# Output projection's right half in groups (0, 1), (2), (3), and the last tile's expert rows accumulated in DRAM onto a stored shift

## The chip, the cores and the metric

The kernel runs on one core of a Trainium2 chip. A core has a matrix engine (PE), three engines for elementwise work (DVE, ACT, POOL), a queue engine that issues most transfers here (SP), and 16 DMA engines. Each engine works through its own list of instructions in order, and waits on semaphores where it needs another one's result. The metric is the device time of one launch, in microseconds (us); the time before is the median of three runs.

## What is computed

One layer with a conditioning vector c: a token mixer (convolution, gated recurrence, linear attention) whose output goes through a projection `w_out`, and then a mixture of 16 experts, of which each token uses two. 512 tokens, width 1024, float32.

```python
        mod = (c_act @ w_ada[l] + b_ada[l])[:, None, :]
        sh1, sc1, gt1, sh2, sc2, gt2 = jnp.split(mod, 6, axis=-1)
        h = rms_norm(x, g_mix[l]) * (1.0 + sc1) + sh1
        x = x + gt1 * token_mix(h, w_in[l], conv_dw_w[l], conv_dw_b[l], conv_ln_g[l], conv_ln_b[l],
...
        h = rms_norm(x, g_ffn[l]) * (1.0 + sc2) + sh2
        x = x + gt2 * hier_moe(h, w_route_group[l], b_route_group[l], w_route_expert[l],
                               b_route_expert[l], w_gate[l], w_up[l], w_down[l])
    return rms_norm(x, g_final)
```

`token_mix` ends in `mixed @ w_out`, the output projection. `hier_moe` picks one of four groups by `h @ w_rg`, two of its four experts by `h @ w_re`, and adds their outputs `(silu(h w_gate) * (h w_up)) w_down`, weighted.

## The kernel before

**Tiles and stages.** The 512 tokens stand in four tiles of 128 (NT = 4). A first stage normalises x and runs the mixer; up to some 220 us this is not touched. Then come the output projection with the routing, from about 200 to 262 us, and the experts, to the end.

**Output projection.** Its 1024 output columns are done in two halves. The left half (`ps0`) is done for all four tiles. The right half is done by `project(tiles, units)`: it goes through the eight steps of 128 input columns, at each step three matmuls for each tile in `tiles` (`mm3`, L84 to L86: products of high and low parts), the last three steps together tile by tile. After each step it may run one of `units`, that is, other work that is written in between. `yres(i, half, ps)` multiplies a finished half by the gate (tile yr, L981) and adds it to the residual xt(i) (L982), both on DVE.

**Routing of a tile.** `route_half(i, hf)` scales half a tile of xt into xa (L997, DVE), transposes it by PE (tile ph2, L1001), copies it on ACT (h2t, L1003), multiplies it by the routing weights on PE (pl, L1006) and copies that on ACT (pls, L1008). `route(i)` does this for the right half, stores xt(i) in DRAM (xo_rows, L1029, SP), squares and sums xt(i) on ACT (L1031, result in ss2), takes the power -1/2 of the mean (a scaling on DVE L116, a power on POOL L117), sums the four partial logits on PE (L1035) and writes the tile's logits lg (L1036, DVE).

**Rows for the experts.** `rows(i)` makes h of tile i, that is xa times the root mean square factor plus the shift sh2, and stores it in DRAM as h2_dram (h2_rows in the lists, h_rows in the trace; L1045, SP). For tiles 0 to 2 that is one DVE instruction (L1041); for the last tile it is a multiplication on ACT (L1043) and an addition on POOL (L1044):

```python
        else:
            nc.scalar.mul(xa, xa, ss2[:, i:i + 1])
            nc.gpsimd.tensor_tensor(xa, xa, sh2, ALU.add)
        nc.sync.dma_start(h2_dram[i * P:(i + 1) * P, :], xa)
```

**From logits to experts.** With all four tiles' lg, DVE finds each token's group and experts by maxima and one-hot masks (`first_max`, L1103 to L1110), PE counts positions (L1134), and a list of row numbers is made for each expert (sidx, L134). POOL then gathers an expert's rows from DRAM (`gather`, L1142, tile gat), which needs h2_dram of all tiles and the expert's sidx. DVE also ranks the experts by load (L1175 to L1186), and all engines branch on whether one is overfull (L1290, L1291). After the branch PE transposes the gathered rows of the first expert (L1383), and the expert stage runs.

**Experts and their weights.** An expert has three weight matrices; all are streamed from DRAM in 96 chunks of 1 MB (`load_chunk`, L966, issued on SP) over a ring of 17 slots, in the order of use. A chunk's load waits until its slot is free and until the load three before it has landed (AHEAD = 3). Eight experts are computed one at a time in three-pass matmuls (L84 to L86), the other eight in pairs (L1414, L1460). The results are added to xo_rows in DRAM by indexed accumulating DMAs from POOL (L1086).

**What sets the order.** The source gives the order in which work is written; a scheduler then sets each engine's list. The lists around the change stand below as they come out.

Of the kernel before, what the change touches and what calls it, by code (L numbers as in the profile page):

```python
# [13 lines left out]
ALU = mybir.AluOpType  # L14
# [3 lines left out]
P = 128  # L18
D = 1024
T = 512  # L20
NT = T // P
# [27 lines left out]
def trunk_kernel(  # L49
# [7 lines left out]
    nc = tc.nc  # L57
# [9 lines left out]
    h2_dram = nc.dram_tensor("h2_rows", (T, D), F32, kind="Internal").ap()  # L67
# [9 lines left out]
    def big(name):  # L77
        return pbank("pz", 6, name)

    def small(name):  # L80
        return pbank("ps", 2, name)

    def mm3(ps, lh, ll, rh, rl, start, stop):
        nc.tensor.matmul(ps, lh, rh, start=start, stop=False)  # L84
        nc.tensor.matmul(ps, lh, rl, start=False, stop=False)  # L85
        nc.tensor.matmul(ps, ll, rh, start=False, stop=stop)  # L86
# [28 lines left out]
    def rstd_of(dst, src, n):  # L115
        nc.vector.tensor_scalar(dst, src, 1.0 / n, EPS, ALU.mult, ALU.add)  # L116
        return nc.gpsimd.tensor_tensor(dst, dst, mhalf[:, 0:dst.shape[1]], ALU.pow)  # L117
# [256 lines left out]
    for kd in range(KD):  # L374
# [10 lines left out]
        if kd in (1, 2, 4):  # L385
            n = kd // 2 + 1
# [74 lines left out]
    def t512(name, tag="t", bufs=8):  # L461
        return tmp.tile([P, T], F32, tag=tag, bufs=bufs, name=name)
# [317 lines left out]
    def row_tile(name):  # L780
        return modp.tile([P, D], F32, tag="row", name=name)

    def bcast(dst, row):
        nc.sync.dma_start(dst, row.rearrange("(o n) -> o n", o=1).broadcast_to((P, D)))
# [4 lines left out]
    gt1, a2, sh2 = (row_tile(n) for n in ("gt1", "a2", "sh2"))  # L789
# [4 lines left out]
    def mod_rows():  # L794
        nc.sync.dma_start(wr[:, :, 0:4], w_route_group[0].rearrange("(k p) g -> p k g", p=P))
        for g in range(4):
            nc.sync.dma_start(wr[:, :, 4 + 4 * g:8 + 4 * g],
                              w_route_expert[0, g].rearrange("(k p) e -> p k e", p=P))
        nc.sync.dma_start(br[:, 0:4], b_route_group)
        nc.sync.dma_start(br[:, 4:20], b_route_expert[0].rearrange("g e -> (g e)").rearrange("(o g) -> o g", o=1))  # L800
        bcast(gt1, mod_dram[0])
        bcast(a2, mod_dram[2])
        bcast(sh2, mod_dram[1])
        nc.sync.dma_start(sh2r, mod_dram[1].rearrange("(k p) -> k p", p=P))
        for hf in range(2):
            cols = slice(hf * 512, hf * 512 + 512)
            gffn = t512(f"gffn{hf}")
            nc.sync.dma_start(gffn, g_ffn[:, cols].broadcast_to((P, 512)))
            nc.vector.scalar_tensor_tensor(a2[:, cols], a2[:, cols], 1.0, gffn, ALU.add, ALU.mult)
# [85 lines left out]
    def w_right():  # L895

        for n, kd in enumerate(ksteps):
            if kd not in right:
                if n < 6:
                    if n % 2 == 0:  # L900
                        both_ = ring0[n // 4].tile([P, 2, 2, 512], F32R, tag="raw", name=f"parts_o{kd}")
                    hi, lo = both_[:, n % 2, 0, :], both_[:, n % 2, 1, :]
                else:
                    hi = wop.tile([P, 512], F32R, tag="wh", name=f"hi_r{kd}")
                    lo = wop.tile([P, 512], F32R, tag="wl", name=f"lo_r{kd}")
                split(hi, lo, rawo[1, kd])
                right[kd] = hi, lo
            yield kd, *right[kd]
# [69 lines left out]
    def yres(i, half, ps):  # L978
        t = late.tile([P, 512], F32, tag="yr", bufs=1, name=f"yr{half}{i}")
        cs_ = slice(half * 512, half * 512 + 512)  # L980
        nc.vector.tensor_tensor(t, ps, gt1[:, cs_], ALU.mult)  # L981
        nc.vector.tensor_tensor(xt[i][:, cs_], xt[i][:, cs_], t, ALU.add)  # L982
# [10 lines left out]
    def route_half(i, hf):  # L993

        xa = xas[i]
        cols = slice(hf * 512, hf * 512 + 512)
        nc.vector.tensor_tensor(xa[:, cols], xt[i][:, cols], a2[:, cols], ALU.mult)  # L997
        pt = big(f"ph2{i}{hf}")
        for kk in range(4):
            k = hf * 4 + kk  # L1000
            nc.tensor.transpose(pt[:, kk * P:(kk + 1) * P], xa[:, k * P:(k + 1) * P], ident)  # L1001
        h2t = late.tile([P, 4, P], F32, tag="h2t", bufs=2, name=f"h2t_{i}{hf}")
        nc.scalar.copy(h2t, pt.rearrange("p (k t) -> p k t", k=4))  # L1003
        pl = small(f"pl{i}{hf}")
        for q in range(4):
            nc.tensor.matmul(pl[32 * q:32 * q + 32, 0:P], wr[:, hf * 4 + q, :], h2t[:, q, :], start=True, stop=True)  # L1006
        pls[i, hf] = late.tile([P, P], F32, tag=f"pls{hf}", bufs=1 if hf else NT, name=f"pls{i}{hf}")
        nc.scalar.copy(pls[i, hf], pl[:, 0:P])  # L1008

    def project(tiles, units=()):  # L1010

        py = {i: big(f"py1{i}") for i in tiles}
        units, held = list(units), []
        for n, step in enumerate(w_right()):
            held.append(step)
            if KD - 3 <= n < KD - 1:
                continue
            for i in tiles:
                for kd, hi, lo in held:
                    mm3(py[i], mth[:, kd, i * P:(i + 1) * P], mtl[:, kd, i * P:(i + 1) * P],  # L1020
                        hi, lo, kd == first, kd == final)
            held = []
            if units:
                units.pop(0)()
        return py

    def route(i):
        route_half(i, 1)
        nc.sync.dma_start(xo_dram[i * P:(i + 1) * P, :], xt[i])  # L1029
        junk = late.tile([P, D], BF16, tag="junk2", bufs=1, name=f"junk2{i}")  # L1030
        nc.scalar.activation(junk, xt[i], AF.Square, accum_out=ss2[:, i:i + 1])  # L1031
        rstd_of(ss2[:, i:i + 1], ss2[:, i:i + 1], D)
        pl2 = small(f"pl2{i}")
        for hf in range(2):
            nc.tensor.matmul(pl2[:, 0:20], pls[i, hf], sel, start=(hf == 0), stop=(hf == 1))  # L1035
        nc.vector.scalar_tensor_tensor(lg[:, i, :], pl2[:, 0:20], ss2[:, i:i + 1], lgc, ALU.mult, ALU.add)  # L1036

    def rows(i):
        xa = xas[i]
        if i < NT - 1:  # L1040
            nc.vector.scalar_tensor_tensor(xa, xa, ss2[:, i:i + 1], sh2, ALU.mult, ALU.add)  # L1041
        else:
            nc.scalar.mul(xa, xa, ss2[:, i:i + 1])  # L1043
            nc.gpsimd.tensor_tensor(xa, xa, sh2, ALU.add)  # L1044
        nc.sync.dma_start(h2_dram[i * P:(i + 1) * P, :], xa)  # L1045

    for i in range(NT):
        yres(i, 0, ps0[i])
    py = project((0, 1))
    for i in range(2):  # L1050
        yres(i, 1, py[i])
    py = project((2, 3), [lambda i=i: [route_half(n, 0) for n in (i, i + 1)] for i in (0, 2)]
                 + [lambda i=i: route(i) for i in (0, 1)])
    for i in range(nring - 8, EARLY):
        load_chunk(i)
    for i in (0, 1):
        rows(i)
    for i in range(2, NT):
        yres(i, 1, py[i])
        route(i)  # L1060
    for i in range(2, NT):
        rows(i)
    keep_busy(10)
# [602 lines left out]
```

## Time and profile before

| | |
|---|---|
| median of 3 runs | 544.02 us (541.79 to 544.24) |
| profiled execution, its own time | 539.03 us |
| its span in the trace | 537.3 us |
| PE busy | 505.9 us, 94% |
| DVE busy | 362.5 us, 67% |
| ACT busy | 248.5 us, 46% |
| POOL busy | 90.0 us, 17% |
| DMA, HBM read | 156.35 MB, 314 GB/s over the span |
| mean granted clock of PE | 0.977 of full speed |

Rows below come from the one profiled execution. Times are us from the start of its span, line numbers are those of the kernel before. "Idle before" in brackets is the time for which an engine stood still ahead of an instruction, with the work that ended it. A q behind an engine's name means its queue: a waiting or issuing instruction, not counted as busy.

### The profile page before, as it was taken

How to read it: one execution, taken by the hardware profiler on the slowest of the kernel's cores; microseconds unless marked ns; L12 is line 12 of the kernel's file. 1: busy time of each engine (PE TensorE's matmuls, PEld its weight loads, DVE VectorE, ACT ScalarE, POOL GpSimd, SP SyncE). 2: the span in 40 equal slices, each digit the busy share in tenths (PEclk: the TensorE clock that was granted, in tenths of full speed). 3: DMA queues.
4: the chain of work that ended last, by engine and by line, in shares of the span. 5: the costliest groups of instructions: out<-in, count | busy, mean ns of one | idle time of the engine just before them, and what ended most of it. 6: DMA issues, size and time to landing. Idle time of an engine off the chain costs nothing. (4 is left out here: it accounts for less than half of the span.)

```text
span 537.3 us, 7963 instructions
## 1 busy us (share of the span) xinstructions
PE 505.9 (94%) x2835; PEld 344.5 (64%) x2835; DVE 362.5 (67%) x654; ACT 248.5 (46%) x397; POOL 90.0 (17%) x126
## 2 busy tenths in 40 slices
PE   8999999999998999996889999999999999999991
PEld 7766766677666887775667778787777353343341
DVE  4644499999988756538799999999899031120237
ACT  5432587496126543225467667777766011000113
POOL 3310414000025100104200211120120110112002
PEclk9999999999999999997599999999999999999997
DMA  8995978747727399368898899999999999999973
GB/s 284 300 344 151 290 252 282 231 155 302 291 77 267 154 359 421 160 234 294 314 351 305 321 371 360 352 375 366 348 391 373 363 412 357 393 365 402 403 323 156
DMA packets 54304, 164.58 MB, mean 306 GB/s; under 512 B 12181, under 2 KB 30881, under 8 KB 39926
## 3 DMA queue, kind: packets, MB, share of 16 engines
q1 hardware_dynamic: 50710, 156.36, 79.1%
q0 software_dynamic: 3552, 7.69, 5.4%
q8 instruction: 23, 0.38, 0.3%
q14 instruction: 19, 0.16, 0.1%
HBM read 156.35 MB, written 12.62 MB: 314 GB/s over the span
## 5 line engine op out<-in xcount | busy, mean ns | idle before, releaser
L509 DVE SCALAR_TENSOR_TENSOR cacc<-upad,vt,cacc 128x512 f32<-128x512 f32 x60 | 43.0, 753 | 0.1
L1537 DVE SCALAR_TENSOR_TENSOR sact<-pup,swt,sact 128x512 f32<-128x512 f32 x12 | 8.9, 745 | 49.7 <-PE pup L1414 49.7
L90 DVE TENSOR_TENSOR ml_u<-raw_u,mh_u 128x1024 fp32r<-128x1024 f32 x32 | 39.1, 1224 | 3.9 <-ACT mh_u L89 3.8
L89 ACT CAST mh_g<-raw_g 128x1024 fp32r<-128x1024 f32 x32 | 33.5, 1051 | 17.0 <-PE pga L86 12.3
L90 DVE TENSOR_TENSOR ml_g<-raw_g,mh_g 128x1024 fp32r<-128x1024 f32 x32 | 38.3, 1219 | 1.3 <-ACT mh_g L89 1.1
L89 ACT CAST mh_u<-raw_u 128x1024 fp32r<-128x1024 f32 x32 | 33.6, 1050 | 11.4 <-PE pga L86 9.2
L90 DVE TENSOR_TENSOR ml_d<-raw_d,mh_d 128x1024 fp32r<-128x1024 f32 x26 | 31.7, 1223 | 4.0 <-ACT mh_d L89 3.6
L1142 POOL DMA_INDIRECT gat<-h_rows,sidx x12 | 13.5, 1122 | 120.9 <-PE pgt L1383 68.9
L1460 PE MATMUL pd<-raw_d,ht 128*64 128x512 f32 x128 | 32.7, 599 | 0.9 <-DMA raw_d<-in_w_down_dram 0.9
L89 ACT CAST mh_d<-raw_d 128x1024 fp32r<-128x1024 f32 x26 | 27.3, 1049 | 8.1 <-PE pup L86 6.1
L1414 PE MATMUL pup<-raw_u,xh 128*64 128x512 f32 x128 | 29.4, 595 | 0.8 <-DMA raw_u<-in_w_up_dram 0.8
L1487 DVE TENSOR_TENSOR ye<-pd,gt 128x512 f32<-128x512 f32 x22 | 15.0, 690 | 20.9 <-PE pd L1460 19.4
L1414 PE MATMUL pga<-raw_g,xh 128*64 128x512 f32 x128 | 28.3, 594 | 0.0
L84 PE MATMUL pga<-mh_g,xh 128*128 128x512 f32 x64 | 27.6, 431 | 0.5 <-ACT xh L89 0.5
L85 PE MATMUL pup<-ml_u,xh 128*128 128x512 f32 x64 | 25.6, 400 | 1.6 <-DVE ml_u L90 1.5
L85 PE MATMUL pga<-ml_g,xh 128*128 128x512 f32 x64 | 26.2, 410 | 0.6 <-DVE ml_g L90 0.6
L86 PE MATMUL pga<-mh_g,xl 128*128 128x512 f32 x64 | 25.6, 400 | 0.4 <-DVE xl L90 0.4
L84 PE MATMUL pup<-mh_u,xh 128*128 128x512 f32 x64 | 25.8, 403 | 0.0
L86 PE MATMUL pup<-mh_u,xl 128*128 128x512 f32 x64 | 25.2, 394 | 0.0
L1086 POOL DMA_INDIRECT xo_rows<-ye,sidx x8 | 17.1, 2138 | 36.7 <-DVE ye L1487 36.7
L1460 PEld LDWEIGHTS pd<-raw_d,ht 128*64 128x64 f32 x128 | 10.6, 136 | 19.6 <-issue 16.0
L1426 ACT COPY ht<-pht 128x512 f32<-128x512 f32 x4 | 2.3, 587 | 42.6 <-PE pht L1422 42.6
(405 smaller groups left out, 1267.7 us busy)
## 6 DMA issues: line engine op xcount, KB each, us to landing
raw_g<-in_w_gate_dram SPq DMA_DIRECT2D x32, 1024.0 KB
raw_u<-in_w_up_dram SPq DMA_DIRECT2D x32, 1024.0 KB
raw_d<-in_w_down_dram SPq DMA_DIRECT2D x32, 1024.0 KB
wb<-in_w_ada_dram SPq DMA_DIRECT2D x16, 1024.0 KB
wa<-in_w_ada_dram SPq DMA_DIRECT2D x8, 512.0 KB
wa<-in_w_ada_dram SPq DMA_DIRECT2D x4, 1024.0 KB
raw_o<-in_w_out_dram SPq DMA_DIRECT2D x8, 512.0 KB
xin<-in_x_dram SPq DMA_DIRECT2D x4, 512.0 KB
```

The costliest lines, as they stand in the source:

```text
L84: nc.tensor.matmul(ps, lh, rh, start=start, stop=False)
L85: nc.tensor.matmul(ps, lh, rl, start=False, stop=False)
L86: nc.tensor.matmul(ps, ll, rh, start=False, stop=stop)
L89: one = nc.scalar.copy(hi, src)
L90: two = nc.vector.tensor_tensor(lo, src, hi.bitcast(F32), ALU.subtract)
L509: nc.vector.scalar_tensor_tensor(cacc[:, h, :], upad[:, h, t:t + T], w, cacc[:, h, :], ALU.mult, ALU.add)
L1086: nc.gpsimd.indirect_dma_start(out=xo_dram, out_offset=bass.IndirectOffsetOnAxis(ap=si, axis=0), in_=y, in_offset=None, bounds_check=T - 1 ...
L1142: return g, nc.gpsimd.indirect_dma_start(out=g, out_offset=None, in_=h2_dram, in_offset=bass.IndirectOffsetOnAxis(ap=sidx[:, e:e + 1], axi ...
L1414: nc.tensor.matmul(ps[rows_of(a)], xh[:, k, rows_of(a)], raws[used[0] + a][:, kk, :], start=(k == 0), stop=(k == KD - 1))
L1460: nc.tensor.matmul(ps[hf][rows_of(a)], ht[:, k, rows_of(a)], raws[used[0] + k // 2 * 2 + a][:, k % 2, cols(hf)], start=(k == 0), stop=(k = ...
L1487: nc.vector.tensor_tensor(y[:, cols], ps[hf], gt2[:, cols], ALU.mult)
L1537: nc.vector.scalar_tensor_tensor(sa, pu, swt[:, u:u + 1], sa, ALU.mult, ALU.mult)
```

## The change

Three things. The shift sh2 is stored once in the last tile's part of h2_dram, early (`mod_rows`). The last tile's rows are no longer completed on POOL and stored by SP: after ACT's multiplication POOL issues a DMA that adds them onto what stands in DRAM. And the right half is projected for tile 2 and tile 3 one after the other, with other units of routing written between their steps; yres(2, 1) is written ahead of tile 3's projection, and the logits of tile 2 inside it.

```diff
--- before.py
+++ after.py
@@ -801,6 +801,8 @@
         bcast(gt1, mod_dram[0])
         bcast(a2, mod_dram[2])
         bcast(sh2, mod_dram[1])
+
+        nc.sync.dma_start(h2_dram[(NT - 1) * P:, :], sh2)
         nc.sync.dma_start(sh2r, mod_dram[1].rearrange("(k p) -> k p", p=P))
         for hf in range(2):
             cols = slice(hf * 512, hf * 512 + 512)
@@ -1039,25 +1041,31 @@
         xa = xas[i]
         if i < NT - 1:
             nc.vector.scalar_tensor_tensor(xa, xa, ss2[:, i:i + 1], sh2, ALU.mult, ALU.add)
+            nc.sync.dma_start(h2_dram[i * P:(i + 1) * P, :], xa)
         else:
             nc.scalar.mul(xa, xa, ss2[:, i:i + 1])
-            nc.gpsimd.tensor_tensor(xa, xa, sh2, ALU.add)
-        nc.sync.dma_start(h2_dram[i * P:(i + 1) * P, :], xa)
+            nc.gpsimd.dma_start(h2_dram[i * P:(i + 1) * P, :], xa, accum_op=ALU.add)
 
     for i in range(NT):
         yres(i, 0, ps0[i])
     py = project((0, 1))
     for i in range(2):
         yres(i, 1, py[i])
-    py = project((2, 3), [lambda i=i: [route_half(n, 0) for n in (i, i + 1)] for i in (0, 2)]
-                 + [lambda i=i: route(i) for i in (0, 1)])
+    def nothing():
+        pass
+
+    def left_halves(*tiles):
+        return lambda: [route_half(n, 0) for n in tiles]
+
+    py = project((2,), [nothing, left_halves(0, 1), nothing, left_halves(2, 3), nothing, lambda: route(0)])
+    yres(2, 1, py[2])
+    py = project((3,), [nothing, lambda: route(1), nothing, nothing, nothing, lambda: route(2)])
     for i in range(nring - 8, EARLY):
         load_chunk(i)
     for i in (0, 1):
         rows(i)
-    for i in range(2, NT):
-        yres(i, 1, py[i])
-        route(i)
+    yres(3, 1, py[3])
+    route(3)
     for i in range(2, NT):
         rows(i)
     keep_busy(10)
```

The lists of instructions around it follow; tile names carry the tile and half (xa2 is tile 2; pl22 the summed logits of tile 2; yr13 the right half of tile 3).

DVE, from the left-over work of tile 2 to the last logits, before:

```order
L981 TENSOR_TENSOR yr12_2532<-py12_2364,gt1_1825 128x512
L982 TENSOR_TENSOR xt2_2217<-xt2_2217,yr12_2532 128x512
L997 TENSOR_TENSOR xa2_2271<-xt2_2217,a2_1826 128x512
L981 TENSOR_TENSOR yr13_2559<-py13_2365,gt1_1825 128x512
L116 TENSOR_SCALAR ss2_2268<-ss2_2268 128x1
L982 TENSOR_TENSOR xt3_2218<-xt3_2218,yr13_2559 128x512
L997 TENSOR_TENSOR xa3_2272<-xt3_2218,a2_1826 128x512
L1041 SCALAR_TENSOR_TENSOR xa2_2271<-xa2_2271,ss2_2268,sh2_1827 128x1024
L1036 SCALAR_TENSOR_TENSOR lg_2267<-pl22_2555,ss2_2268,lgc_1830 128x20
L116 TENSOR_SCALAR ss2_2268<-ss2_2268 128x1
L1036 SCALAR_TENSOR_TENSOR lg_2267<-pl23_2582,ss2_2268,lgc_1830 128x20
L1103 TENSOR_REDUCE m1_2628<-lg_2267 128x16
```

and after:

```order
L999 TENSOR_TENSOR xa2_2272<-xt2_2218,a2_1826 128x512
L1043 SCALAR_TENSOR_TENSOR xa1_2271<-xa1_2271,ss2_2269,sh2_1827 128x1024
L116 TENSOR_SCALAR ss2_2269<-ss2_2269 128x1
L1038 SCALAR_TENSOR_TENSOR lg_2268<-pl21_2504,ss2_2269,lgc_1830 128x20
L983 TENSOR_TENSOR yr13_2560<-py13_2477,gt1_1825 128x512
L1043 SCALAR_TENSOR_TENSOR xa2_2272<-xa2_2272,ss2_2269,sh2_1827 128x1024
L1038 SCALAR_TENSOR_TENSOR lg_2268<-pl22_2546,ss2_2269,lgc_1830 128x20
L984 TENSOR_TENSOR xt3_2219<-xt3_2219,yr13_2560 128x512
L999 TENSOR_TENSOR xa3_2273<-xt3_2219,a2_1826 128x512
L116 TENSOR_SCALAR ss2_2269<-ss2_2269 128x1
L1038 SCALAR_TENSOR_TENSOR lg_2268<-pl23_2583,ss2_2269,lgc_1830 128x20
L1111 TENSOR_REDUCE m1_2628<-lg_2268 128x16
```

The rows of tile 2 (L1041, now L1043) and its logits (lg from pl22) stood behind xt3 and xa3, and now stand ahead of them; the work of tiles 0 and 1 that used to come earlier is now between that of tile 2.

ACT, over the last tiles' squares (junk), copies and the multiplication of xa3, before:

```order
L1031 ACTIVATE junk22_2551,ss2_2268<-xt2_2217 128x1024
L1003 COPY h2t_21_2541<-ph221_2536 128x512
L1031 ACTIVATE junk23_2578,ss2_2268<-xt3_2218 128x1024
L1008 COPY pls21_2548<-pl21_2543 128x128
L1003 COPY h2t_31_2568<-ph231_2563 128x512
L1008 COPY pls31_2575<-pl31_2570 128x128
L1043 ACTIVATE xa3_2272<-xa3_2272,ss2_2268 128x1024
L89 CAST mh_g000_2793<-raw_g00_2245 128x1024
```

and after:

```order
L1005 COPY h2t_11_2490<-ph211_2485 128x512
L1010 COPY pls11_2497<-pl11_2492 128x128
L1005 COPY h2t_21_2532<-ph221_2527 128x512
L1010 COPY pls21_2539<-pl21_2534 128x128
L1033 ACTIVATE junk23_2579,ss2_2269<-xt3_2219 128x1024
L1005 COPY h2t_31_2569<-ph231_2564 128x512
L1046 ACTIVATE xa3_2273<-xa3_2273,ss2_2269 128x1024
L1010 COPY pls31_2576<-pl31_2571 128x128
L89 CAST mh_g000_2793<-raw_g00_2246 128x1024
```

The multiplication of xa3 (L1043, now L1046) stood behind the copy pls31 and now stands ahead of it; the copy pls21 stood behind the square of tile 3 and now stands ahead.

SP, the stores of xt (xo_rows) and of the rows (h2_rows) among the weight loads, before:

```order
L966 DMA raw_g20_2524<-in_w_gate_dram 128x2048
L1045 DMA h2_rows<-xa0_2269 128x1024
L966 DMA raw_g21_2526<-in_w_gate_dram 128x2048
L1045 DMA h2_rows<-xa1_2270 128x1024
L1029 DMA xo_rows<-xt2_2217 128x1024
L966 DMA raw_u20_2780<-in_w_up_dram 128x2048
L1029 DMA xo_rows<-xt3_2218 128x1024
L1045 DMA h2_rows<-xa2_2271 128x1024
L1045 DMA h2_rows<-xa3_2272 128x1024
L966 DMA raw_u21_2782<-in_w_up_dram 128x2048
L966 DMA raw_d10_2784<-in_w_down_dram 128x2048
```

and after:

```order
L1044 DMA h2_rows<-xa0_2270 128x1024
L1031 DMA xo_rows<-xt2_2218 128x1024
L968 DMA raw_g20_2552<-in_w_gate_dram 128x2048
L968 DMA raw_g21_2554<-in_w_gate_dram 128x2048
L1044 DMA h2_rows<-xa1_2271 128x1024
L1031 DMA xo_rows<-xt3_2219 128x1024
L1044 DMA h2_rows<-xa2_2272 128x1024
L968 DMA raw_u20_2780<-in_w_up_dram 128x2048
L968 DMA raw_u21_2782<-in_w_up_dram 128x2048
L968 DMA raw_d10_2784<-in_w_down_dram 128x2048
```

The store of xa3 on SP is gone, the two loads behind it have no store to wait for any more, and the two loads raw_g20 and raw_g21 stand behind more stores than before.

## Rows read from the trace of the kernel before

**Rows 1.** Windows by stage: stretch, its us, busy us of each engine, PE clock, DMA share, GB/s.

```profile
180.00:188.00 8.00, 8.00 (x48) 7.89 (x47) 5.64 (x10) 6.02 (x10) 0.00 (x0) 1.00 0.01 3
...
242.00:250.00 8.00, 6.80 (x48) 5.69 (x49) 6.45 (x16) 6.54 (x11) 5.28 (x5) 0.79 0.96 311
285.00:385.00 100.00, 99.92 (x502) 78.26 (x501) 93.86 (x108) 72.78 (x86) 17.09 (x10) 1.00 0.96 354
```

**Rows 2.** The chain that ended last: start us, us, who.

```profile
486.73 8.76 DMA raw_u<-in_w_up_dram
```

**Rows 3.** SP's waits from 400 to 425 us: us in total, times, longest.

```profile
SPq L966 <- PE pga L1414: 3.1, 1, 3.1
```

**Rows 4.** Timeline, SP, POOL and PE at the gathers: start us, us, engine, line.

```profile
250.42 0.32 SPq L1045 DMA_DIRECT2D h_rows<-xa  x1
...
255.95 1.18 POOL L1142 DMA_INDIRECT gat<-h_rows,sidx  x1 [4.41 <-DVE cnt L1156]
...
260.78 0.34 SPq L966 DMA_DIRECT2D raw_d<-in_w_down_dram  x1
...
262.73 1.52 PE L1383 MATMUL pgt<-ident,gat 128*128 128x128 f32 x6 [0.87 <-DVEq L1291]
```

**Rows 5.** Timeline of PE at the end of the projection.

```profile
241.56 0.39 PE L86 MATMUL py<-hi_r,mtl 128*128 128x512 f32 x1
...
243.83 0.40 PE L1035 MATMUL pl<-sel,pls 128*128 128x20 f32 x2
244.20 0.66 PE L1001 MATMUL ph<-ident,xa 128*128 128x128 f32 x4
...
245.53 0.43 PE L1006 MATMUL pl<-h2t,wr 128*32 128x128 f32 x8 [0.28 <-ACT h2t L1003]
```

**Rows 6.** Timeline of DVE, from tile 3's half to the one-hots.

```profile
242.00 0.68 DVE L981 TENSOR_TENSOR yr<-py,gt 128x512 f32<-128x512 f32 x1
...
242.72 0.69 DVE L982 TENSOR_TENSOR xt<-xt,yr 128x512 f32<-128x512 f32 x1
243.45 0.69 DVE L997 TENSOR_TENSOR xa<-xt,a 128x512 f32<-128x512 f32 x1
244.57 1.28 DVE L1041 SCALAR_TENSOR_TENSOR xa<-xa,ss,sh 128x1024 f32<-128x1024 f32 x1 [0.43 <-POOL ss L117]
...
245.93 0.14 DVE L116 TENSOR_SCALAR ss<-ss 128x1 f32<-128x1 f32 x1
247.12 0.24 DVE L1036 SCALAR_TENSOR_TENSOR lg<-pl,ss,lgc 128x20 f32<-128x20 f32 x1 [1.05 <-PE pl L1035]
...
247.79 0.17 DVE L1105 TENSOR_TENSOR oh_g<-lg,gmax 128x16 f32<-128x16 f32 x1
...
248.09 2.33 DVE L1107 TENSOR_TENSOR oh_g<-oh_g,neg 128x16 f32<-128x16 f32 x1
```

**Rows 7.** Timeline of ACT in the same stretch.

```profile
243.50 1.06 ACT L1031 ACTIVATE junk<-xt 128x1024 bf16<-128x1024 f32 x1
...
244.89 0.59 ACT L1003 COPY h2t<-ph 128x512 f32<-128x512 f32 x1
246.08 0.27 ACT L1008 COPY pls<-pl 128x128 f32<-128x128 f32 x1 [0.60 <-PE pl L1006]
246.73 1.15 ACT L1043 ACTIVATE xa<-xa,ss 128x1024 f32<-128x1024 f32 x1 [0.39 <-POOL ss L117]
```

**Rows 8.** Timeline of POOL in the same stretch.

```profile
246.15 0.55 POOL L117 TENSOR_TENSOR ss<-ss,mhalf 128x1 f32<-128x1 f32 x1 [0.71 <-DVE ss L116]
247.95 2.44 POOL L1044 TENSOR_TENSOR xa<-xa,sh 128x1024 f32<-128x1024 f32 x1 [1.26 <-ACT xa L1043]
```

**Rows 9.** Indexed accumulating DMAs: issue ns, then issue to landing.

```profile
L1086 POOL DMA_INDIRECT xo_rows<-ye,sidx x8: 1586/2312/2362, 302.4 to 438.2; - x8
...
DMA to landing us min/median/max: 7.4/11.2/12.9
```

## The prediction

> **What bounds the kernel now.** I read the windows by stage first, to see which engine is full where. From 285 to 385 us the matrix engine works 99.92 of 100 us [rows 1], so in the expert stage PE sets the pace, and whatever delays its first expert instruction delays all that follows. Next the chain that ended last: it stays on PE until a weight load takes over at 486.73 us [rows 2], so the end waits for DMA. That could swallow a shift of the expert stage, so I looked at what the weight loads wait for before that. As late as 400 to 425 us a load waits up to 3.1 us for a slot that a PE matmul (L1414) still holds [rows 3]. Slots are freed by PE, so loads issued up to there move with PE, and the DMA-bound tail moves with the loads. I therefore pass a shift of the start of the expert stage on to the end one to one.
>
> So the question is when PE begins the first transposes of gathered rows (L1383). Before, that is at 262.73 us, and the row names DVE's branch (L1291) as its releaser, not the gather: the load on SP that waits for the first gather went out at 260.78, so the gathered rows were there 1.95 us early [rows 4]. The start hangs on DVE's routing chain: last logits (L1036) at 247.12, one-hots, positions, gather lists, ranking, branch. The instructions behind that last lg are in the same order before and after, so two dates decide: when the last lg starts, and when the gather of the first expert lands.
>
> **The projection itself** costs the same: PE has as many matmuls, the same three-pass groups, and the last one, tile 3's, ends at 241.95 [rows 5]. Splitting (2,3) into (2) and (3) takes tile 2 away earlier, but tile 2 is not what the last lg waits for. DVE's yr of tile 3 can start at 242.00 as before [rows 6]; I call this the zero point. PE hardly paused there before, so I see nothing to gain ahead of it.
>
> **The tail, where the order moves things the wrong way.** Before, DVE ran yr(3), xt(3), xa(3) back to back (242.00, 242.72, 243.45) and only then the rows of tile 2 (1.28 us) [rows 6]; the last lg started 5.12 us after the zero point. After, DVE is given yr(3), rows of tile 2, lg(2), and only then xt(3), xa(3). An engine works in order, so tile 3 waits for both. Tile 2's lg needs: PE's last transposes of tile 2 (0.66, they stand behind tile 3's last matmul), ACT's copy (0.59), PE's logits (0.43), ACT's copy pls (0.27), PE's two matmuls with sel (0.40), lg (0.24) [rows 5 to 7]. From 241.95 that ends at 244.54, later than yr(3) and the rows (242.00 + 0.68 + 1.28 = 243.96). So xt(3) starts at 244.54 and not at 242.72, 1.8 us late.
>
> From there: xt(3) 0.69 to 245.23; ACT's square of xt(3) 1.06 to 246.29; DVE's scaling 0.14 and POOL's power 0.55 to 246.98 [rows 6 to 8]. After, ACT has its multiplication of tile 3's rows (1.15) ahead of the copy pls(3) (0.27); before it came behind. It waits for that power, so pls(3) ends at 248.40, PE's two matmuls at 248.80, and lg(3) can start at 248.8 at the earliest. Some ten hand-overs between engines lie on this way; one takes 0.05 (245.48 to 245.53 between ACT's copy and PE's logits, [rows 5, 7]), all about 0.5. I take 249.3 against 247.12: **2.2 us lost** (1.7 without them).
>
> **What is gained there.** In before, DVE's oh_g of 128x16 (L1107) took 2.33 us where an instruction of the same shape beside it (L1105) took 0.17 [rows 6]. In just that time, 247.95 to 250.39, POOL added the shift to tile 3's rows, 2.44 us [rows 8]. DVE stood still for that addition, 2.16 us on the path. The Trainium skill, "SBUF — State Buffer", section "Who interferes with whom", says that a VectorE instruction with two SBUF inputs and a GpSimd instruction that reads SBUF exclude each other for the whole instruction; by that rule the stall goes with the addition, and the row agrees. After, POOL does no addition and the stall has no cause left: **2.2 us gained**. In its place POOL issues an accumulating DMA. Its issue may hold DVE up in turn: not at all, or for its whole length, 1.18 us by the gather's row [rows 4]; I take 0, since POOL then adds nothing. Together the DVE chain comes out at 0 (from -0.5 to +1.2): the edit of the rows pays for the new order, and no more.
>
> **The accumulating DMA.** Before, the last tile's rows left SP as a plain store at 250.42, and were in DRAM long before the gather was asked for at 255.95 [rows 4]. After, ACT ends the multiplication at about 248.5 (246.98 + 1.15, and hand-overs), and POOL sends 512 KB in accumulating packets, starting at about 248.6. The first gather waits for its landing, on POOL's queue, and the second gather stands behind it there. Nothing in before shows a plain accumulating DMA of that size. The nearest rows are the indexed accumulating DMAs of the expert outputs, of at most the same 512 KB (128 rows of 4 KB): 7.4, 11.2 and 12.9 us (least, median, most) from issue to landing, of which POOL's issue itself is 2.3 [rows 9]. The lower bound is the gather of 512 KB, 4.8 us (260.78 - 255.95, [rows 4]), which only reads DRAM. DMA is busy 0.96 in 242 to 250 us [rows 1], and two weight chunks that stood on SP behind the store at 250.42 now leave ahead of the accumulation; that speaks for the upper rows. The gather's issue is 1.18 against 2.3, so I take the median less 1.1, 10.1 us: landing at 258.7 (bounds 253.4 and 261.5). The gather then leaves at 258.7, lands at 258.7 + 4.8 = 263.5, and PE starts there and not at 262.73. It costs 0.8 us. The point from which the landing counts is 257.9 (262.73 - 4.83); at any earlier landing the DVE chain hides it.
>
> The Trainium skill, "DMA: Bandwidth & Descriptors", section "Anatomy of one DMA — SWDGE (gpsimd) path", puts a DMA from GpSimd at 2.0 us plus its bytes by 436 GB/s, which is 3.2 us for 512 KB (an estimate by that page); the accumulation would land near 251.8 and the sum would be 0 and not +0.8. The accumulating rows here, never under 7.4 us, disagree, so the rows stand.
>
> **Edits at no cost.** The new store of the shift (512 KB on SP) comes where DMA is 0.01 busy, 180 to 188 us [rows 1]; its issue is some 0.3 us, ahead of a weight chunk that went out at 188 and is used only past 262. Without that idle time it would be 1.5 us (512 KB at the 354 GB/s of 285 to 385). On SP two weight chunks move behind the stores of xt(0) to xt(2) and of tile 0's rows, so they leave some microseconds later; both belong to the third expert, and nothing reads them before PE starts the first at 262.73. If the cover were gone it would be at most one load of 1 MB, 3.0 us at that rate. The plain store of tile 3's rows on SP goes.
>
> **Sum.** Profiled execution 539.03 us: -2.2 + 2.2 + 0.8 = 539.8. The median of the three runs, 544.02, lies 5.0 above the profiled execution, and even the fastest, 541.79, lies 2.8 above. The shift is the same in each, so the median becomes 544.8.
>
> **Rivals.**
> *The new order costs nothing (faster).* If lg(2) is ready when DVE gets to it and ACT's multiplication overlaps other waits, the 2.2 us are not lost, and the gain on DVE remains, provided the accumulation lands by 255.7. For it: the tile alone lets tile 2's first work run under tile 3's matmuls. Against it: tile 2's last transposes still stand behind tile 3's last matmul on PE. It gives 544.0 - 2.2 = 541.8; even that is within 0.5%.
> *The accumulation lands late (slower).* At the most of the rows, 12.9 us, it lands at 261.5, the gather at 266.3, PE starts 3.6 us late: 547.6. It decides from a landing later than 257.9 on, and is over 0.5% from 260.6 on (257.9 + 2.7). For it: DMA is full and the accumulating rows are long. Against it: the issue is simpler than the indexed one.
> *The shift does not reach the end.* If the DMA stream alone sets the end, the start of the experts doesn't matter: 544.0. Against it stand the waits on slots [rows 3].
>
> **How the numbers follow.** A measurement of this kernel tells about 0.5% (2.7 us) from no change. Forecast (DVE chain equal, landing by 260): 0.62. Order free: 0.13, of which I put 0.08 beyond 0.5%, for a further gain from the clock or the emptier SP queue that I can't see. Late accumulation: 0.20, of which 0.18 beyond 0.5%. No effect: 0.05. So faster 0.08, same 0.74, slower 0.18. The range reaches from the free order and the 0.5% below no change (541.8 and 541.3) to the latest landing, 547.6; it leaves out the 0.08 below and a little above.
>
> **What would show it.** In the changed profile: DVE runs tile 2's rows and lg(2) before xt(3), and the last lg starts 7 us or more after yr(3) (right) or near 5 us (wrong). No DVE instruction of the one-hots takes over 0.5 us (right); if one still takes 2 us, POOL's DMA issue blocks DVE, and the result is 2 us slower. The gather's wait on POOL names the accumulating DMA, and ends after 256 us; PE's first transposes wait for the gather and not for DVE's branch. If the last projection matmul moved by over 0.5 us, the step on the projection is wrong; if PE's start and the total moved by different amounts, the one-to-one step is.

## The result, and the profile of the changed kernel

The changed kernel takes 545.27 us (median of 19 runs, 543.30 to 548.59) against 542.09 us for the kernel before (19 runs beside them): a ratio of 1.0062, 95% interval 1.0046 to 1.0078, that is 3.4 us slower (2.5 to 4.2). The forecast was 544.8, a shift of +0.8 us on a base of 544.02. The time lies in the range, and the sign is right, but the two numbers lie close together by luck: the median of the three runs of before known then was 1.9 us above the median of the 19. The shift itself was four times the forecast. It is outside "within 0.5%", which had 0.74, on the slower side, which had 0.18.

| | before | changed |
|---|---|---|
| span of the profiled execution | 537.3 | 542.6 |
| last projection matmul ends | 241.95 | 242.92 |
| last lg starts, after that end | 5.17 | 7.36 |
| first gather issued, after that end | 14.00 | 19.04 |
| PE starts the experts, after that end | 20.78 | 24.21 |

The profiled execution of the changed kernel was 1 us late before the new order began: the scaling of the first squares (L116) starts at 226.61 before and 227.53 after, and from there to the end of the projection it is 15.34 us before and 15.39 after. Most of that (0.64 us) is there already at an ACT cast at 175.57 before and 176.21 after, ahead of the stored shift at 180.83. So all times below are counted from the end of the last projection matmul, called S. PE starts 3.43 us later after S; the comparison of all runs gives 3.4.

PE, at the end of the projection and where the experts start (start us, us, engine, line; what answers to [rows 4, 5]):

```profile
242.53 0.39 PE L86 MATMUL py<-hi_r,mtl 128*128 128x512 f32 x1
242.76 0.60 PE L1003 MATMUL ph<-ident,xa 128*128 128x128 f32 x4
...
246.96 0.66 PE L1003 MATMUL ph<-ident,xa 128*128 128x128 f32 x4 [1.66 <-DVE xa L999]
248.29 0.65 PE L1008 MATMUL pl<-h2t,wr 128*32 128x128 f32 x8 [0.68 <-ACT h2t L1005]
...
267.13 1.09 PE L1391 MATMUL pgt<-ident,gat 128*128 128x128 f32 x4 [4.09 <-DMA gat<-h_rows,sidx]
```

The last line stands for the last of [rows 4]: there its releaser (the work named in brackets, which ended the wait) is DVE's branch, here it is the gather, waited for 4.09 us.

DVE in the same stretch (what answers to [rows 6]):

```profile
242.96 0.69 DVE L983 TENSOR_TENSOR yr<-py,gt 128x512 f32<-128x512 f32 x1 [1.70 <-PE py L86]
243.57 1.27 DVE L1043 SCALAR_TENSOR_TENSOR xa<-xa,ss,sh 128x1024 f32<-128x1024 f32 x1
245.34 0.24 DVE L1038 SCALAR_TENSOR_TENSOR lg<-pl,ss,lgc 128x20 f32<-128x20 f32 x1 [0.49 <-PE pl L1037]
245.49 0.68 DVE L984 TENSOR_TENSOR xt<-xt,yr 128x512 f32<-128x512 f32 x1
...
250.28 0.24 DVE L1038 SCALAR_TENSOR_TENSOR lg<-pl,ss,lgc 128x20 f32<-128x20 f32 x1 [2.73 <-PE pl L1037]
...
251.26 0.17 DVE L1115 TENSOR_TENSOR oh_g<-oh_g,neg 128x16 f32<-128x16 f32 x1
...
262.64 0.32 DVE L1194 TENSOR_REDUCE ranked<-named 1x13 int32<-1x169 f32 x1
```

Tile 2's rows and lg(2) hold up xt(3), and the last lg is late; the one-hot that took 2.33 us takes 0.17. DVE's ranking, the end of its chain, starts at S + 19.72, against S + 19.43 before (261.38). The two halves of the change cancel on DVE to 0.29 us, nearly as forecast. The rest goes with a wait of DVE that the kernel before did not have: 0.38 us (at L1145) for PE's counts, which stood on PE behind matmuls on ones (L147) that took 4.61 us here and 3.80 before.

ACT, at the last multiplication and the last copy (what answers to [rows 7]):

```profile
248.20 1.15 ACT L1046 ACTIVATE xa<-xa,ss 128x1024 f32<-128x1024 f32 x1
249.26 0.24 ACT L1010 COPY pls<-pl 128x128 f32<-128x128 f32 x1
```

The copy pls(3) starts as the multiplication ends; PE's logits, which it copies, had ended at 248.94 (248.29 + 0.65, above).

POOL, and SP with the weight loads (q: an issue, not work):

```profile
249.65 0.96 POOL L1047 DMA_DIRECT2D h_rows<-xa  x1 [1.48 <-ACT pls L1010]
...
261.96 1.15 POOL L1150 DMA_INDIRECT gat<-h_rows,sidx  x1 [10.77 <-DVE which L1187]
...
247.10 1.92 SPq L968 DMA_DIRECT2D raw_u<-in_w_up_dram  x2
249.12 18.23 SPq L968 DMA_DIRECT2D raw_d<-in_w_down_dram  x2
```

The view of the accumulating line (L1047), its last row:

```profile
DMA to landing us min/median/max: 11.4/11.4/11.4
```

So the accumulation is asked for at S + 6.73 and has landed at 261.01, behind three weight loads that left at 247.1 to 249.1 (raw_u20, raw_u21, raw_d10; the second raw_d of the last row is a later load, which waits for the gather). POOL does nothing in between but a memset of 0.1 us. The releaser that the gather's row names, a small DVE instruction, is only what ended last in that moment; the gather's list (sidx) was ready at 256.56, and the only other thing that it waits for is the accumulation.

Windows by stage (stretch, its us, busy us of PE, its weight loads, DVE, ACT, POOL, then clock, DMA share, GB/s; compare [rows 1]):

```profile
180.00:188.00 8.00, 8.00 (x45) 7.54 (x44) 5.34 (x10) 5.26 (x8) 0.00 (x0) 1.00 0.23 92
...
250.00:255.00 5.00, 4.86 (x31) 4.70 (x31) 4.10 (x28) 2.11 (x4) 0.71 (x2) 0.54 1.01 330
...
285.00:385.00 100.00, 98.98 (x495) 77.05 (x494) 94.31 (x111) 71.47 (x85) 18.41 (x11) 1.00 0.96 354
```

DMA is full while the accumulation waits; the store of the shift went into time that was idle (a DMA share of 0.23 here, 0.01 in [rows 1]); the expert stage is as full as before, so the late start is not made up.

### The profile page after: what moved, and what is told of

It reads as the page before. It is cut to its first block, busy times and chain, and to the rows that moved or that the text cites. A ratio compares the mean times of both kernels' runs of the same rounds, so it can differ in the third digit from the quotient of the medians.

```text
span 542.6 us, 7968 instructions
## 1 busy us (share of the span) xinstructions
PE 507.3 (93%) x2835; PEld 345.8 (64%) x2835; DVE 360.1 (66%) x654; ACT 248.5 (46%) x397; POOL 88.5 (16%) x126
## 4 chain that ended last, share of the span: by engine, by line
PE 63%; issue 11%; DMA 10%; DVE 10%; ACT 3%; POOL 2%; SPq 1%; POOLq 0%; DVEq 0%; ACTq 0%
PE pga L1422 4%; PE pup L1422 3%; DMA raw_u<-in_w_up_dram 3%; DMA raw_d<-in_w_down_dram 3%; PE pd L1468 3%; PE py L86 3%; PE py L85 3%; PE py L84 2%; PE pga L86 2%; PE pd L84 2%; PE pga L85 2%; PE pga L84 2%; PE pd L85 2%; PE pup L85 2%; PE pd L86 2%
## 5 line engine op out<-in xcount | busy, mean ns | idle before, releaser
L89 ACT CAST mh_u<-raw_u 128x1024 fp32r<-128x1024 f32 x32 | 33.6, 1050 | 11.2 <-PE pga L86 9.0
```

What stands on the lines that cost most here:

```text
L89: one = nc.scalar.copy(hi, src)
```

## The experiments

Each was compared with runs of the kernel before on the same chip. "PE start" is the first transpose of gathered rows, after S, from the profile of each kernel (before 20.78, changed 24.21). Ratios are turned into us with 542.4, the median of before beside them (542.95 beside the plain store and beside the last rows on DVE in the order of the change).

**The order alone.** Built on the changed kernel; rows as before, no stored shift.

```diff
-        nc.sync.dma_start(h2_dram[(NT - 1) * P:, :], sh2)
...
-            nc.gpsimd.dma_start(h2_dram[i * P:(i + 1) * P, :], xa, accum_op=ALU.add)
+            nc.gpsimd.tensor_tensor(xa, xa, sh2, ALU.add)
+        nc.sync.dma_start(h2_dram[i * P:(i + 1) * P, :], xa)
```

> The tile split alone: the last tile's rows are finished by ACT and POOL and stored by SP as before, and no shift is stored early. Theory (the accumulating DMA costs the time, the order only as much as the stall gave): the last logits start 7.3 us after yr(3) as in the changed kernel, and POOL's addition again holds DVE up, but for only about 1.3 us, because it starts before the one-hots; the DVE chain ends 1.3 to 2.2 us later than before, the gather is not waited for, time +1.3 to +2.2 us (ratio 1.0024 to 1.004). Rival (the order alone is the whole loss): +3.4 us, 1.006. Rival (the order costs nothing): 0.

Measured: 1.0047 (1.0026 to 1.0068), +2.5 us; PE start 22.88, +2.1. POOL, DVE and PE of this kernel:

```profile
248.92 2.35 POOL L1045 TENSOR_TENSOR xa<-xa,sh 128x1024 f32<-128x1024 f32 x1 [1.40 <-ACT xa L1044]
...
249.77 0.24 DVE L1037 SCALAR_TENSOR_TENSOR lg<-pl,ss,lgc 128x20 f32<-128x20 f32 x1 [3.13 <-PE pl L1036]
...
250.30 1.06 DVE L1112 TENSOR_TENSOR oh_e<-lg,m 128x64 f32<-128x64 f32 x1
...
264.90 1.95 PE L1390 MATMUL pgt<-ident,gat 128*128 128x128 f32 x8 [1.70 <-DMA gat<-h_rows,sidx]
```

SP's weight loads of this kernel, then of before, and the landing of this kernel's first gather:

```profile
251.71 1.22 SPq L967 DMA_DIRECT2D raw_u<-in_w_up_dram  x2
253.02 12.10 SPq L967 DMA_DIRECT2D raw_d<-in_w_down_dram  x2
```

```profile
250.83 0.38 SPq L966 DMA_DIRECT2D raw_u<-in_w_up_dram  x1
251.31 9.80 SPq L966 DMA_DIRECT2D raw_d<-in_w_down_dram  x2
```

```profile
DMA to landing us min/median/max: 7.5/7.5/7.5
```

The last lg is late (7.75 us after S), and POOL's addition stops DVE for the part of it that is left, 0.83 us, until it ends at 251.27; by a plain sum DVE's chain is 1.27 us late (ranking at S + 20.70). But PE waited for the gather, which the theory had ruled out: it took 7.5 us to land against 4.8 before. The new order on SP puts three weight loads shortly ahead of it and the old one two (the second raw_d of each row waits for the gather); raw_u20, the third, left at S - 0.14 before. So the order has two prices, one on DVE and one on the gather.

**The accumulation alone.** Built on the kernel before, its order kept.

```diff
+        nc.sync.dma_start(h2_dram[(NT - 1) * P:, :], sh2)
...
-            nc.gpsimd.tensor_tensor(xa, xa, sh2, ALU.add)
-        nc.sync.dma_start(h2_dram[i * P:(i + 1) * P, :], xa)
+            nc.gpsimd.dma_start(h2_dram[i * P:(i + 1) * P, :], xa, accum_op=ALU.add)
```

> The stored shift and the accumulating DMA alone, projection in the order of before. Theory: no one-hot on DVE takes over 0.5 us, so the DVE chain is 2.2 us earlier; but the accumulation starts at about 248, needs some 11.4 us as in the changed kernel, the gather leaves about 0.9 us behind its landing and needs 5 us: PE starts the experts at about 265.3 instead of 262.73, time +2.6 us (1.005). Rival (the order is the cause): the accumulation is hidden, time -2.2 us (0.996).

Measured: 1.0027 (1.0010 to 1.0045), +1.5 us; PE start 22.29, +1.5. DVE, POOL and PE of this kernel:

```profile
248.55 0.17 DVE L1109 TENSOR_TENSOR oh_g<-oh_g,neg 128x16 f32<-128x16 f32 x1
...
248.86 0.96 POOL L1047 DMA_DIRECT2D h_rows<-xa  x1 [1.48 <-ACT xa L1046]
...
259.87 1.15 POOL L1144 DMA_INDIRECT gat<-h_rows,sidx  x1 [7.37 <-DMA raw_d<-in_w_down_dram]
...
264.92 1.94 PE L1385 MATMUL pgt<-ident,gat 128*128 128x128 f32 x8 [4.67 <-DMA gat<-h_rows,sidx]
```

Its weight loads, and the landing of the accumulation:

```profile
246.97 0.44 SPq L968 DMA_DIRECT2D raw_u<-in_w_up_dram  x1
247.52 17.61 SPq L968 DMA_DIRECT2D raw_d<-in_w_down_dram  x2
```

```profile
DMA to landing us min/median/max: 10.1/10.1/10.1
```

DVE's chain is 2.28 us earlier than before (ranking at S + 17.15), and PE gains nothing of it: it waits 4.67 us for a gather that waits for the accumulation (landed at 258.92; the weight load in the gather's row is what ended last by the profile). The gain on DVE is real and hidden. The expected +2.6 us was 1.1 too much: it took the 11.4 us of the changed kernel, and here the landing took 10.1, with two weight loads just ahead (S + 4.35 and 4.90) and not three, since raw_u20 left at S - 0.14 as before.

**Weight loads behind the accumulation.** Built on the changed kernel.

```diff
     for i in range(EARLY, HELD):
-        load_chunk(i)
+        load_chunk(i, *added)
```

`added` holds the accumulating DMA; `load_chunk` makes the load wait for it.

> The changed kernel, but the three weight loads (raw_u20, raw_u21, raw_d10) that leave just ahead of the accumulating DMA now wait for its landing. Theory (it shares DMA with 3 MB of weights): issue to landing falls from 11.4 to 5 to 7 us, the gather is there before DVE's branch, PE starts 20.8 to 21.1 us after the last projection matmul instead of 24.2, time +0 to +0.5 us against before (1.000 to 1.001), if the pause of the weight stream is made up later. Rival (accumulating into DRAM is slow by itself): landing stays near 11 us, PE starts as in the changed kernel, time +3.4 us or more.

Measured: 1.0067 (1.0039 to 1.0095), +3.6 us; PE start 23.64, +2.9. The accumulation's landing, and the gather's:

```profile
DMA to landing us min/median/max: 5.8/5.8/5.8
```

```profile
DMA to landing us min/median/max: 9.1/9.1/9.1
```

Half of the theory held: without loads ahead the accumulation lands in 5.8 us and not in 11.4. The expected time was wrong all the same. The three loads now left between the landing and the gather, and the gather took 9.1 us: the same 3 MB only stood ahead of another DMA.

**Weight loads behind the gather.** Built on the changed kernel.

```diff
     for i in range(EARLY, HELD):
-        load_chunk(i)
+        load_chunk(i, gathers[0][1])
```

> The changed kernel, but the three weight loads that leave ahead of the accumulating DMA now wait until the first gather has landed. Theory (both the accumulation and the gather are slow only because 3 MB of weights lie ahead of them): the accumulation needs about 6 us, the gather about 5, PE waits for DVE's branch again and starts 21.1 us after the last projection matmul (before 20.8, changed 24.2), time +0.3 us (1.0005), since the order costs 2.2 us and the stall gave them back. Rival (the weight stream has no slack): PE starts as early, but the pause in the weights, 8 to 13 us, comes back as waits later, time +2 us or more.

Measured: 1.0012 (0.9990 to 1.0034), +0.7 us; PE start 21.15, +0.4. POOL and PE of this kernel:

```profile
256.32 1.15 POOL L1150 DMA_INDIRECT gat<-h_rows,sidx  x1 [5.84 <-DVE cnt L1164]
...
263.08 1.95 PE L1391 MATMUL pgt<-ident,gat 128*128 128x128 f32 x8 [0.87 <-DVEq L1299]
```

With accumulation (6.0 us) and gather (4.2 us) both ahead of the loads, the releaser is DVE's branch again, as in [rows 4]. What is left is the DVE chain, 2.2 lost and 2.2 gained. The three loads leave 14 to 15 us later after S, and that costs nothing that can be told here.

**A plain store in the accumulation's place.** Built on the changed kernel; the shift is left out of the last tile's rows.

```diff
-            nc.gpsimd.dma_start(h2_dram[i * P:(i + 1) * P, :], xa, accum_op=ALU.add)
+            nc.gpsimd.dma_start(h2_dram[i * P:(i + 1) * P, :], xa)
```

> The changed kernel with a plain store in place of the accumulating one, at the same place on POOL's queue; the shift is left out of the last tile's rows. Theory (the long landing comes from the weight loads ahead, not from adding): issue to landing stays at 9 us or more, against 11.4 accumulating, PE starts 22 to 24 us after the last projection matmul, time +1.5 to +3 us against before (1.003 to 1.006). Rival (adding in DRAM is what takes long): landing within 5 to 6 us, PE starts at about 21.5, time +0.5 us (1.001).

Measured: 1.0038 (1.0009 to 1.0067), +2.1 us; PE start 22.86, +2.1. The store's landing:

```profile
DMA to landing us min/median/max: 10.0/10.0/10.0
```

Adding in DRAM accounts for 1.4 of the 11.4 us, of which 0.3 is POOL's longer issue (0.96 and 0.67 us). The rest is a DMA of 512 KB from POOL behind the same three weight loads.

**The last rows on DVE, order of before.** Built on the kernel before.

```diff
-        if i < NT - 1:
-            nc.vector.scalar_tensor_tensor(xa, xa, ss2[:, i:i + 1], sh2, ALU.mult, ALU.add)
-        else:
-            nc.scalar.mul(xa, xa, ss2[:, i:i + 1])
-            nc.gpsimd.tensor_tensor(xa, xa, sh2, ALU.add)
+        nc.vector.scalar_tensor_tensor(xa, xa, ss2[:, i:i + 1], sh2, ALU.mult, ALU.add)
```

> The kernel before, with the last tile's rows made by one DVE instruction as for the other tiles; no ACT multiplication, no POOL addition, no accumulation. Theory (POOL's addition stalls DVE for 2.2 us on the path that starts the experts): the instruction of 1.28 us delays the last logits by 0.9 us, the stall of 2.16 us goes, PE starts about 1.2 us earlier, time -1.2 us (0.998). Rival (the stall has another cause): one of the one-hots still takes 2 us, time +0.9 us.

Measured: 0.9975 (0.9949 to 1.0000), -1.4 us; PE start 19.47, -1.3. DVE and PE of this kernel:

```profile
246.91 1.28 DVE L1040 SCALAR_TENSOR_TENSOR xa<-xa,ss,sh 128x1024 f32<-128x1024 f32 x1 [0.66 <-POOL ss L117]
...
249.08 0.17 DVE L1103 TENSOR_TENSOR oh_g<-oh_g,neg 128x16 f32<-128x16 f32 x1
...
261.60 1.94 PE L1379 MATMUL pgt<-ident,gat 128*128 128x128 f32 x8 [0.87 <-DVEq L1287]
```

The instruction of 1.28 us costs 0.8 (last lg at S + 5.98 and not 5.17), the stall of 2.16 is gone, and this kernel's median is below both others'. Its interval just touches 1.

**The last rows on DVE, order of the change.** Built on the changed kernel with the rows of the kernel above and no stored shift.

> The tile split in the order of the changed kernel, with the last tile's rows by one DVE instruction and a store on SP: no ACT multiplication ahead of the copy pls(3), no addition on POOL, no accumulation. Theory: the wait of xt(3) for lg(2) still costs 1.8 us, but lg(3) no longer waits for the multiplication and starts at about 6.6 us after yr(3); without a stall DVE's chain ends about 0.8 us earlier than before; the gather, with three loads ahead, needs 7 us and sets PE's start at 20.2 to 20.6 us (before 20.8), time -0.2 to -0.6 us (0.999). Rival (the split itself is a gain once the last rows are cheap): PE starts at 19.5 or earlier, time -1.3 us or better (0.9975), as with the order of before.

Measured: 1.0018 (0.9990 to 1.0047), +1.0 us; PE start 21.73, +0.95. Both expectations missed. Neither stall nor accumulation is in this kernel, so with the same rows the order of the change costs 2.3 us (PE start +0.95 against -1.31 with the order of before). The last lg starts at S + 7.58 although ACT's multiplication is gone. PE's rows say why, and the windows of this kernel and of before (columns as above, the clock third from the end):

```profile
246.16 1.12 PE L1002 MATMUL ph<-ident,xa 128*128 128x128 f32 x4 [1.66 <-DVE xa L998]
247.95 0.66 PE L1007 MATMUL pl<-h2t,wr 128*32 128x128 f32 x8 [0.68 <-ACT h2t L1004]
```

```profile
244.00:246.00 2.00, 0.40 (x2) 0.30 (x2) 1.47 (x4) 0.64 (x2) 0.00 (x0) 0.97 0.95 320
246.00:248.00 2.00, 1.17 (x8) 0.77 (x12) 0.61 (x3) 1.15 (x3) 1.46 (x2) 0.50 0.98 393
```

```profile
244.00:246.00 2.00, 1.68 (x16) 1.00 (x16) 1.57 (x4) 1.39 (x4) 1.44 (x2) 1.00 0.90 233
246.00:248.00 2.00, 1.94 (x9) 1.94 (x10) 0.92 (x9) 1.54 (x3) 0.59 (x2) 0.55 0.92 297
```

PE was busy 0.40 of the 2 us from 244, since xt(3) and xa(3) come late on DVE. Then the granted clock is 0.50, that is 1.2 and not 2.4 GHz, and transposes take 1.12 us and not 0.66, logits 0.66 and not 0.43 [rows 5]. The fall itself does not come from the order alone: before, the clock is 0.55 in the same stretch, after 1.68 busy of 2 us. But there tile 3's transposes and logits (244.20 and 245.53 [rows 5]) lie ahead of the fall, and here behind it. Why it falls when it does, no run shows. The gather, with three loads ahead, took 7.3 us.

**Tile 2's routing one step earlier, two ways.** Built on the changed kernel; once with the rows on DVE, and once with the accumulation kept and the loads behind the gather, as above.

```diff
-    py = project((3,), [nothing, lambda: route(1), nothing, nothing, nothing, lambda: route(2)])
+    py = project((3,), [nothing, lambda: route(1), nothing, nothing, lambda: route(2)])
```

> The tile split, with tile 2's routing written one step earlier, so that its transposes stand between tile 3's matmuls; the last tile's rows by one DVE instruction and a store on SP, no accumulation. Theory: DVE goes from yr(3) to xt(3) without a wait, the last logits start about 5.1 us after yr(3), the instruction for the last rows fits into the wait for them, no one-hot stalls; DVE's ranking ends some 2.1 us earlier than before and PE starts 18.7 to 19.2 us after the last projection matmul, if the gather, now with three loads ahead, does not land later. Time -1.6 to -2.1 us (0.996 to 0.997). Rival (the loads ahead of the gather decide): PE waits for the gather, starts at 20 us or later, time -0.8 us or worse.

> The changed kernel with both costs taken away: tile 2's routing one step earlier, and the three weight loads behind the first gather. Theory: the last logits start 5.1 to 5.5 us after yr(3), no stall on DVE, accumulation landed about 11 us after the last projection matmul and hidden, PE starts at 18.7 to 19.2 us (before 20.8), time -1.6 to -2.1 us (0.996 to 0.997). Rival (the pause of the weight stream costs): PE starts as early but the time is that of before or more.

Measured: with rows on DVE 0.9993 (0.9975 to 1.0011), -0.4 us, PE start 18.86 after S; with the accumulation 1.0002 (0.9980 to 1.0025), +0.1 us, PE start 19.38. PE starts 1.9 and 1.4 us earlier after S, the first as expected, the second 0.2 us later than expected (its last lg at S + 5.95 and not 5.1 to 5.5), and the time hardly moves. So both rivals' times came, but not for their reasons: a wait for the gather still let PE start at 18.86, and a pause of the loads had cost nothing that shows above. The two yr on DVE, of tile 2 and tile 3, show why (the kernel with rows on DVE, then the changed one):

```profile
234.55 0.69 DVE L982 TENSOR_TENSOR yr<-py,gt 128x512 f32<-128x512 f32 x1 [6.91 <-PE py L86]
...
244.31 0.69 DVE L982 TENSOR_TENSOR yr<-py,gt 128x512 f32<-128x512 f32 x1 [0.55 <-PE py L86]
```

```profile
234.60 0.69 DVE L983 TENSOR_TENSOR yr<-py,gt 128x512 f32<-128x512 f32 x1 [6.91 <-PE py L86]
```

The second of the changed kernel, at 242.96, is shown above. From one to the other it is 9.76 us in the kernel with rows on DVE and 8.36 in the changed one. S itself moved by 1.40 us: tile 2's transposes, logits and sums now stand between tile 3's matmuls, on an engine that is full (busy 4.00 of the 4 us from 240 in the kernel with rows on DVE). Less 1.4, the gains are 0.5 and 0.0 us, as measured. The expectations left out that S moves.

**The stored shift alone.** Built on the kernel before, the store of the shift added and later overwritten.

> The kernel before, with the shift also stored in the last tile's part of the rows at 181 us, and overwritten later by that tile's rows as before. Theory: the store falls into 8 us of idle DMA and costs nothing, time 0 (0.999 to 1.001). Rival (it delays the weight loads behind it on SP): +0.3 to +1 us.

Measured: 0.9997 (0.9976 to 1.0017), -0.2 us (-1.3 to +0.9). The interval alone does not rule out the smaller costs of the rival; the traces show no delay of the weight load behind the store: from the ACT cast named above to that load it is 12.67 us before (175.57 to 188.24) and 12.68 here (176.61 to 189.29), and over all traces 12.67 to 13.28 without the store and 12.67 to 13.19 with it.

**All together.** A start of the experts moves the time one to one (PE start and S from one trace of each kernel, the ratio from all its runs):

| kernel | PE start after S, against before | S moved | ratio, in us |
|---|---|---|---|
| changed | +3.43 | 0 | +3.4 |
| order alone | +2.10 | 0 | +2.5 |
| accumulation alone | +1.51 | 0 | +1.5 |
| loads behind the accumulation | +2.86 | 0 | +3.6 |
| loads behind the gather | +0.37 | 0 | +0.7 |
| plain store from POOL | +2.08 | 0 | +2.1 |
| rows on DVE, order of before | -1.31 | 0 | -1.4 |
| rows on DVE, order of the change | +0.95 | 0 | +1.0 |
| stored shift alone | +0.21 | 0 | -0.2 |
| routing earlier, rows on DVE | -1.92 | +1.4 | -0.4 |
| routing earlier, loads behind the gather | -1.40 | +1.4 | +0.1 |

The largest difference between the sum of the middle columns and the last is 0.7 us, within the intervals.

## Why the prediction was right, and where it was too small

**One to one to the end: right.** The table shows it for eleven kernels, so the rival that the shift does not reach the end falls.

**The projection: right.** 15.34 and 15.39 us from the same point to S.

**The order, 2.2 us lost: right.** The faster rival, an order that costs nothing, falls with it. The last lg moved from S + 5.17 to S + 7.36, 2.19 us. xt(3) started at S + 2.57 against the 2.59 of the working, and the copy pls(3) did wait for ACT's multiplication. What the working left out is PE's lower clock. In the changed kernel it came too late to add to this: the transposes still took 0.66 us, and the logits, at 0.65, were ready 0.3 us before the copy. With the same list on ACT, where the clock fell before the transposes (the order alone, and the loads behind the accumulation), these took 1.12 and 1.11 us and the last lg started at S + 7.75. In the kernel with the rows on DVE in this order, without the multiplication, the slower transposes and logits (0.46 and 0.23 us more) made the last lg late, at S + 7.58.

**The stall, 2.2 us gained: right.** The one-hot took 0.17 us; in the accumulation alone DVE's chain ended 2.28 us earlier; and where POOL's addition was kept but came at another moment, it stopped another instruction for as long as it still ran. POOL's issue of the DMA held DVE up nowhere that shows.

**The accumulation, +0.8 us: the step that was too small.** Its mechanism was right: PE waits for the gather, the gather for the accumulation. In us, against the working:

| | forecast | measured |
|---|---|---|
| issue after S | 6.65 | 6.73 |
| issue to landing | 10.1 | 11.36 |
| landing to the gather's issue | 0 | 0.95 |
| gather's issue to landing | 4.83 | 5.04 |
| PE start behind it | 0 | 0.13 |
| PE start after S | 21.58 | 24.21 |

Two terms were too small. The 0.95 us from landing to issue was put at nothing, though it was to be seen in the trace of before: sidx for the first gather was ready at 255.06, and the gather went out at 255.95 [rows 4]; there it lay beside DVE's chain, here it lies on the path. And 10.1 us to landing became 11.4. The working counted two weight loads that now leave ahead of the accumulation; a third, raw_u20, moved too, from S - 0.14 to S + 4.18. With two just ahead, the last of them 1.3 us, the landing took 10.1 us in the accumulation alone; with three, the last 0.5 us ahead, it took 11.4. The third load fits the difference, but no run moved it alone. That a median of other DMAs less 1.1 us for the issue came so near to the first of these is luck; with the median left whole (11.2) and the 0.95 the sum would have been 544.02 + 2.8.

Counted from S, the accumulation landed at S + 18.09, which is 260.04 in the working's times: at the edge of its "landing by 260", and short of the 260.6 from which it put the result beyond 0.5%. The result was beyond 0.5% all the same, since both this point and the 257.9 of the slower rival left the 0.95 out.

The Trainium skill, "DMA: Bandwidth & Descriptors", section "Anatomy of one DMA — SWDGE (gpsimd) path", gives 2.0 us and the bytes by 436 GB/s, an estimate of 3.2 us for this DMA. Measured: 11.4 behind weight loads and 5.8 to 6.0 without; the measurement decides, and here the estimate is too low in both.

**The edits at no cost.** The stored shift costs nothing that the runs or the load behind it show. The two weight loads that the working saw move (raw_g20, raw_g21) left at S - 5.40 and S - 3.74, and nothing in the table above asks for a cost of theirs. It missed the move of raw_u20, and it did not ask what the loads do to the gather. Three loads shortly ahead cost the gather 2.2 to 2.7 us in the kernels without an accumulation (7.0, 7.3 and 7.5 us against 4.8).

## What to carry to other kernels

A DMA that is put on the path is priced with the transfers that are in flight when it leaves, and with the time from its landing to the next issue on its queue; the same three weight loads cost the accumulation some 5 us (11.4 against 5.8 to 6.0), and moved behind it they cost the gather 4 to 5 (9.1 against 4.2 to 5.0). An engine that is full gives no free place for work that waited behind it: what tile 2's routing won after S (1.9 and 1.4 us) was lost before it (1.4). Where an off-path engine's addition stalls the engine on the path, the cheapest cure here was to let that engine do the addition itself in one instruction (-1.4 us, with an interval that just touches 0).

## What the runs showed of the hardware

- A gather from POOL goes out 0.9 us behind what it waits for (0.87 to 0.95 in the twelve traces): behind a landing 261.01 to 261.96, 258.92 to 259.87 (the accumulation alone), 258.89 to 259.83 (the plain store); behind its list 255.06 to 255.95 (before) and 253.91 to 254.83 (rows on DVE).
- The time from issue to landing of the first gather, 512 KB, went with the weight loads ahead of it: 4.2 and 4.3 us with none, 4.3 to 5.4 with two, 7.0 to 7.5 with three, 9.1 with three that had just left, and 4.9 to 5.0 where the loads had left 11 to 15 us before.
- PE's granted clock fell from 1.00 to 0.50 in the routing tail: 0.55 in 246 to 248 us before, 0.50 in the same 2 us in the last rows on DVE in the order of the change. Tile 3's transposes, at S + 4.04 in that kernel and in the changed one, took 1.12 us behind the fall and 0.66 ahead of it.
